# Logits of two heads side by side: 64-row products, one head in each half of the array

## The chip, the cores and the metric

The kernel runs on one core of a Trainium2 chip. The metric is the device time of one execution in microseconds (us). The core has a matrix engine (TensorE, PE in the profile, with its weight loads shown apart as PEld), a vector engine (VectorE, DVE), a scalar engine (ScalarE, ACT), a general engine (GpSimd, POOL) and a queue engine that starts transfers (SyncE, SP). Products accumulate in PSUM; everything else works in SBUF. The engines run beside each other and wait for one another by semaphores; each takes its own instructions in order.

## The reference

The kernel computes a trunk of two layers on x of 2048 frames by 1024 channels, in float32. Each layer normalises x, projects it, runs two groups of attention heads beside each other, multiplies each output by its SiLU gate, projects the concatenation and adds the residual.

- Group A (layer 0): differential attention, 4 heads. Each head has two sets of queries and keys of 64 numbers; the output uses softmax 1 minus lambda times softmax 2, with values of 128 numbers. A query sees all chunks up to its own, with a linear distance bias.
- Group B (layer 0): 8 heads of 64 with a forget gate, frame-causal; the logit bias is a difference of cumulated log gates.
- Group C (layer 1): 8 query heads on 2 key heads, a window of 128 frames, with sinks.
- Group D (layer 1): 8 heads of 64; a query sees its own chunk of 64 and the eight before it, with a learned bias by distance.

For A, B and D the core is the same:

```python
s = jnp.einsum("bqhd,bkhd->bhqk", qb, k).astype(jnp.float32) * scale
s = s + cq[..., :, None] - cum[:, :, None, :]
s = jnp.where(tk[None, :] <= tq[:, None], s, -jnp.inf)
p = jax.nn.softmax(s, axis=-1)
return jnp.einsum("bhqk,bkhd->bqhd", p.astype(v.dtype), v)
```

Queries and keys are RMS-normalised per head. The logits must be accurate beyond float16, so the kernel splits each operand into a high and a low float16 part and sums products of parts.

## The kernel before, in words

Frames are cut into 16 blocks of 128. The work is a list of steps, one per unit and block. A unit is one head of A (its two sets of queries and keys count as two heads below), or two heads of B, or two of D; so there are 4 units of A, 4 of B and 4 of D, each with 16 steps. Two units of C and the two output projections (32 steps) stand between and after them.

A step has parts, each a list of pieces with a cost in us that only serves to space them: the projection of its block (24 products of 512 columns: eight blocks of channels, three products of parts each, at lines 242 to 244), the split and transposition of queries and keys (`qk_prep`, lines 253 to 287), the logits with their softmax (`qk_row`, lines 322 to 367, and `exp_row`), and the products of the weights with the values (`heads_av`, line 407, for B and D; line 497 for A). The function `drive` runs these staggered: while step i forms its logits, step i+2 is projected, the transposes of step i+1 finish, and the weights of steps i-1 and i-2 meet the values. `merge` sorts the pieces of one turn by their share of the turn: the logits lie in the first nine tenths; B's and D's head 0 of step i-1 meets its values in the second half and head 1 of step i-2 in the first half; A's step i-2 in the first half. This, with the builder's ordering, sets the order of instructions on each engine. Transfers, the transposes of the weights among them, are started from SyncE's queue.

For queries and keys, `qk_prep` squares and sums, scales, and writes the parts high, low, high for every head (line 272 writes the high part twice on ScalarE, line 273 the low part on GpSimd). Pairs of neighbouring parts are transposed by TensorE: (high, low) of each key head, and (high, low) and (low, high) of each query head, six transposes of 128 columns, at lines 277 and 281; two copies on ScalarE bring keys (line 283) and queries (line 286) to SBUF. A key tile has two slots of 512 columns, one per head, with 64 rows of high parts above 64 rows of low parts. A logit of one head is therefore two products over all 128 rows (line 339): high x high + low x low, and low x high + high x low.

`qk_row` handles one head at a time. Its logits go to a PSUM tile of 1024 columns (two banks; there are two such tiles), in runs of up to four key blocks, which is one key tile. For B a further product with a causal mask follows on the last block (line 342). After up to eight blocks VectorE reduces the tile (line 351): it adds the bias, scales, writes the row to SBUF and keeps the running minimum of the negated logits, which goes on as a start value into the next reduction of the row. When the head's last reduction is issued, `exp_row` (line 374) takes the exponentials, and for B and D `weights_T` (lines 302 and 303) splits them into float16 parts and starts their transposition. Then the second head follows. For A both rows must be there first; VectorE and GpSimd combine them (lines 481 to 484) before `weights_T`. Rows live in six SBUF buffers of 1024 columns, shared with a few other uses.

For 16 key blocks a head has two rows of 1024 columns, so a step takes four of the six row buffers; for up to eight blocks, and always in D (at most five blocks), it has one row and the step takes two.

Of the kernel before, what the change touches and what calls it, by code (L numbers as in the profile page):

```python
# [9 lines left out]
F32 = mybir.dt.float32  # L10
F32R = mybir.dt.float32r
F16 = mybir.dt.float16
BF16 = mybir.dt.bfloat16
I32 = mybir.dt.int32
AF = mybir.ActivationFunctionType
ALU = mybir.AluOpType
# [43 lines left out]
class Trunk:  # L60
# [192 lines left out]
    def qk_prep(self, st, z, nq, nk, gain, kdst, mul=None):  # L253
# [13 lines left out]
        if nk:  # L267
            kn = zn[:, nq:, :]
            nc.gpsimd.tensor_tensor(out=kn, in0=kn, in1=gain[:, None, :].broadcast_to([P, nk, 64]), op=ALU.mult)  # L269

# [51 lines left out]
    def qk_row(self, row_st, q, ks, slot, kb0, m, bias, scale, last=None, diag=False):  # L322


        nc = self.nc
        pieces = []
        row_st["rows"] = []
        state = dict(prev=float(3e38))
        base = kb0 - kb0 % 4
        chunks = [(b, min(8, kb0 + m - b)) for b in range(kb0, kb0 + m, 8)]  # L330

        def mms(b0, b, n, end):
            if b == b0:
                state["ps"] = self.pS.tile([P, 1024], F32, tag="s", name="pss")
            c = (b - base) % 8 * P
            ps = state["ps"][:, c:c + n * P]
            k = ks[b // 4]
            for j in range(2):
                nc.tensor.matmul(ps, q()[:, j, :], k[:, slot, (b % 4) * P:(b % 4 + n) * P], start=(j == 0), stop=(j == 1 and not (end and diag)),  # L339
                                 skip_group_check=diag)  # L340
            if end and diag:
                nc.tensor.matmul(ps[:, n * P - P:], self.idh[:], self.causal[:], start=False, stop=True, skip_group_check=True)

        def row_of(b, n, first, last_chunk):
            if first:
                state["mx"] = self.sm.tile([P, 2], F32, tag="mx", name="mx")
            row = self.ap.tile([P, 1024], F32, tag="row", name="row", bufs=6)
            row_st["rows"].append((row, n))
            c = (b - base) % 8 * P
            mx = state["mx"][:, 0:1] if first else state["mx"][:, 1:2]  # L350
            nc.vector.tensor_tensor_reduce(  # L351
                out=row[:, :n * P], in0=state["ps"][:, c:c + n * P], in1=bias(b, n), op0=ALU.add, op1=ALU.min,
                scale=scale, scalar=state["prev"], accum_out=mx)
            state["prev"] = mx
            if last_chunk:
                self.exp_row(row_st, state["prev"])
                if last is not None:
                    last()
        for ci, (b0, n) in enumerate(chunks):
            lastc = ci == len(chunks) - 1  # L360
            b = b0
            while b < b0 + n:
                e = min((b // 4 + 1) * 4, b0 + n)
                pieces.append((2 * max((e - b) * P * 0.42e-3, 0.056), lambda b0=b0, b=b, e=e, x=lastc and e == b0 + n: mms(b0, b, e - b, x)))
                b = e
            pieces.append((0.0, lambda b0=b0, n=n, f=ci == 0, x=lastc: row_of(b0, n, f, x)))
        return pieces
# [58 lines left out]
    def unit_A(self, h, W, wsc, X):  # L426
# [3 lines left out]
        def mk(tb):  # L430
# [3 lines left out]
            def p():  # L434
# [8 lines left out]
                def post():  # L443
                    z = self.evac(st["z"], 512, wsc())
                    kd = self.ktile(ks, tb)
                    g = self.qk_prep(st, z, 2, 2, self.gA[h], kd)
                    if h == 0:
                        self.forget_gate(st, tb)
                    next(g)
                    vs.append(self.v_split(z[:, 256:384], wsc(), 1))  # L450
                    st["gate"] = self.silu2(z[:, 384:512], self.subg[:])
                    next(g)
                    st["fin"] = g
                return pieces + [(0.34, post)]

            def bias(b, n):
                off = (NT - 1 - tb + b) * P
                return self.distA[:, off:off + n * P]

            def q():  # L460
                self.two_sums(st, False)
                out = []
# [23 lines left out]
                for c in range(2):  # L486
                    out += self.qk_row(st["r"][c], lambda c=c: st["q"][c], ks, c, 0, m, bias, self.sA[:, 1 + h:2 + h], last if c == 1 else None)
                return out
# [28 lines left out]
    def unit_BD(self, kind, u, W, wsc, X):  # L517
# [17 lines left out]
        def mk(tb):  # L535
# [4 lines left out]
            def p():  # L540
# [6 lines left out]
                def post():  # L547
                    z = self.evac(st["z"], 512, wsc())
                    kd = self.ktile(ks, tb)
                    g = self.qk_prep(st, z, 2, 2, self.gB if kind == "B" else self.gD, kd)  # L550
# [8 lines left out]
            def bias(h, b, n):  # L559
                if kind == "D":  # L560
                    off = (5 - m + b - kb0) * P
                    return bias_t[h][:, off:off + n * P]
                return bias_t[b // 8, h][:, :n * P]

            def q():
                self.two_sums(st)
                out = []
# [6 lines left out]
                for h in range(2):  # L574
                    out += self.qk_row(st["r"][h], lambda h=h: st["q"][h], ks, h, kb0, m,
                                       lambda b, n, h=h: bias(h, b, n), (self.sB if kind == "B" else self.sD)[:, 1:2], last if h == 1 else None, kind == "B")
                return out
# [568 lines left out]
```

## Time and profile before

| | |
|---|---|
| median of 3 runs | 2675.35 us (2674.71 to 2675.85) |
| profiled execution | 2674.25 us, span 2672.5 us |
| TensorE busy | 2357.1 us, 88% of the span |
| VectorE busy | 1854.3 us, 69% |
| ScalarE busy | 1861.9 us, 70% |
| GpSimd busy | 1463.9 us, 55% |
| mean granted TensorE clock | 0.963 |

The stages in us from the start of the span: A to about 803, B to 1478, the first output projection to about 1700, C to 2005, D to 2486, the second output projection to the end. Busy shares are means over stages with different limits. A row of a group reads: line, engine, operation, output and inputs by the program's names, shapes, count, then busy time and mean ns of one, then the engine's idle time just before and what ended it. A row of waits reads: who waited for whom, total us, how often, the longest. TensorE's rows overlap each other, since products are pipelined, so their pace is read from the distance of starts in the timeline.

### The profile page before, as it was taken

What the parts mean: (1) busy time and instruction counts of PE and PEld (TensorE: products, weight loads), DVE (VectorE), ACT (ScalarE), POOL (GpSimd) and SP (SyncE); (2) the same over time, 40 slices, a digit from 0 to 9 for tenths busy, and PEclk for the clock granted to TensorE, in tenths of its full rate; (3) what the DMA queues carried; (4) which work ended last, traced back from release to release, by engine and by line L of the source; (5) the groups of instructions that cost most, each with busy time, mean ns of one, the idle gap of its engine ahead of it and who ended that gap; (6) DMA issues with size and microseconds to landing.
All of it is one profiled execution on the core that took longest, in us unless ns stands there. A gap on an engine that the chain in (4) does not pass through costs nothing. (4 is left out here: it accounts for less than half of the span.)

```text
span 2672.5 us, 53354 instructions
## 1 busy us (share of the span) xinstructions
PE 2357.1 (88%) x18448; PEld 1300.2 (49%) x18448; DVE 1854.3 (69%) x5228; ACT 1861.9 (70%) x4289; POOL 1463.9 (55%) x2311
## 2 busy tenths in 40 slices
PE   6778888988889989888995898899999999999799
PEld 2344544545455555445553433565555554555344
DVE  6677888888897867857767544566877676767431
ACT  6676777777777877868777444777987777777420
POOL 4555867777786555645554100656575767576300
PEclk9798999999999999999997999999999999999899
DMA  7756555445356997978879999444666776666983
GB/s 213 185 152 137 123 129 132 96 103 125 93 127 133 186 198 147 210 152 165 169 152 193 268 273 245 144 95 118 146 171 138 174 143 163 142 128 141 247 226 103
DMA packets 888208, 426.67 MB, mean 160 GB/s; under 512 B 785377, under 2 KB 816097, under 8 KB 887937
## 3 DMA queue, kind: packets, MB, share of 16 engines
q1 hardware_dynamic: 887936, 423.27, 69.2%
q8 instruction: 144, 2.36, 0.4%
q14 instruction: 128, 1.04, 0.1%
HBM read 187.68 MB, written 42.01 MB: 86 GB/s over the span
## 5 line engine op out<-in xcount | busy, mean ns | idle before, releaser
L374 ACT ACTIVATE row<-row,mx 128x1024 f32<-128x1024 f32 (+7 forms) x512 | 438.2, 857 | 113.2 <-DVE mx L351 111.1
L339 PE MATMUL pss<-kT,qT 128*128 128x512 f16 (+3 forms) x1728 | 398.1, 347 | 56.3 <-DVE mx L351 49.7
L303 DVE SCALAR_TENSOR_TENSOR ph<-row,ph 128x1024 f16<-128x1024 f32 (+6 forms) x320 | 285.6, 902 | 109.3 <-ACT ph L302 107.3
L242 PE MATMUL z<-w,xr 128*128 128x512 f16 x896 | 346.2, 388 | 16.2 <-DMA xr<-xhl 9.0
L242 PE MATMUL z<-w,x 128*128 128x512 f16 x896 | 342.9, 383 | 11.6 <-DMA x<-xs 10.5
L243 PE MATMUL z<-w,xr 128*128 128x512 f16 x896 | 347.2, 388 | 3.4 <-POOL w L113 1.9
L244 PE MATMUL z<-w,xr 128*128 128x512 f16 x896 | 346.4, 387 | 0.0
L243 PE MATMUL z<-w,x 128*128 128x512 f16 x896 | 342.4, 382 | 0.0
L244 PE MATMUL z<-w,x 128*128 128x512 f16 x896 | 342.2, 382 | 0.0
L121 POOL TENSOR_TENSOR y<-v,mhalf 128x4 f32<-128x4 f32 (+2 forms) x329 | 308.4, 938 | 9.1
L407 PE MATMUL OT<-V,pT 128*128 128x64 f16 x5688 | 237.0, 196 | 79.5 <-DMA pT<-ph 77.4
L407 PEld LDWEIGHTS <-pT 128*128 128x128 f16 x5688 | 215.7, 100 | 147.5 <-DMA pT<-ph 96.9
L302 ACT ACTIVATE ph<-row 128x1024 f16<-128x1024 f32 (+6 forms) x320 | 234.4, 744 | 64.0 <-DMA pT<-ph 59.0
L339 PEld LDWEIGHTS <-qT 128*128 128x128 f16 x1728 | 153.1, 101 | 185.9 <-issue 75.7
L273 POOL TENSOR_TENSOR hl<-zs,hl 128x256 f16<-128x256 f32 (+1 forms) x240 | 177.6, 740 | 101.1 <-ACT hl L272 99.2
L123 DVE TENSOR_TENSOR q<-y 128x4 f32<-128x4 f32 (+2 forms) x329 | 90.6, 276 | 204.3 <-POOL y L121 202.4
L272 ACT ACTIVATE hl<-zs 128x512 f16<-128x512 f32 (+1 forms) x240 | 145.8, 608 | 58.9 <-POOL zs L269 52.9
L250 ACT ACTIVATE zs<-z,sc 128x512 f32<-128x512 f32 (+1 forms) x240 | 158.2, 661 | 25.3 <-PE z L244 25.0
L242 PE MATMUL zo<-w,xm 128*128 128x512 f16 x352 | 137.9, 392 | 31.7 <-DVE res L727 14.0
L176 ACT ACTIVATE wrn<-wrn,lng 128x512 f32<-128x512 f32 (+1 forms) x112 | 78.6, 702 | 108.4 <-DMA wrn<-in_wd_dram 43.3
L497 PE MATMUL OA<-V,pT 128*128 128x128 f16 x1632 | 117.4, 230 | 40.6 <-DMA pT<-ph 34.7
L113 POOL TENSOR_TENSOR w<-wraw,w 128x512 f16<-128x512 f32 x118 | 145.6, 1237 | 11.3 <-ACT w L109 10.6
(225 smaller groups left out, 5562.7 us busy)
## 6 DMA issues: line engine op xcount, KB each, us to landing
x<-xs SPq DMA_DIRECT2D x112, 512.0 KB, 3.8
wraw<-in_w_dram SPq DMA_DIRECT2D x64, 256.0 KB, 3.0
wrn<-in_w_dram SPq DMA_DIRECT2D x56, 256.0 KB, 2.9
x<-in_x_dram SPq DMA_DIRECT2D x16, 512.0 KB, 5.1
xs<-xt SPq DMA_DIRECT2D x16, 512.0 KB, 3.3
mixa<-out SPq DMA_DIRECT2D x128, 64.0 KB, 2.1
biasB<-cumd SPq DMA_DIRECT2D x32, 256.0 KB, 5.1
wrn<-in_wo_dram SPq DMA_DIRECT2D x32, 256.0 KB, 3.3
```

The source lines that it names most:

```text
L121: nc.gpsimd.tensor_tensor(out=y[:], in0=v[:], in1=self.mhalf[:, :n], op=ALU.pow)
L242: nc.tensor.matmul(ps(), xh, wh, start=(kb == 0), stop=False)
L243: nc.tensor.matmul(ps(), xh, wl, start=False, stop=False)
L244: nc.tensor.matmul(ps(), xl, wh, start=False, stop=(kb == KB - 1))
L250: self.nc.scalar.activation(zs[:, :n], z[:, :n], AF.Copy, scale=sc[:, 0:1])
L272: nc.scalar.activation(hl[:, :, 0::2], zn[:, :, None, :].broadcast_to([P, n, 2, 64]), AF.Copy)
L273: nc.gpsimd.tensor_tensor(out=hl[:, :, 1], in0=zn, in1=hl[:, :, 0], op=ALU.subtract)
L302: nc.scalar.activation(hl[:, :n], w, AF.Copy, scale=scale)
L303: nc.vector.scalar_tensor_tensor(out=hl[:, n:2 * n], in0=w, scalar=scale, in1=hl[:, :n], op0=ALU.mult, op1=ALU.subtract)
L339: nc.tensor.matmul(ps, q()[:, j, :], k[:, slot, (b % 4) * P:(b % 4 + n) * P], start=(j == 0), stop=(j == 1 and not (end and diag)), skip_g ...
L374: nc.scalar.activation(row[:, :hm * P], row[:, :hm * P], AF.Exp, scale=-1.0, bias=nmax, accum_out=s[:, i:i + 1])
L407: nc.tensor.matmul(O[:, head], w()[:, a], V()[:, b], start=first and a + b == 0, stop=last and a == 1, skip_group_check=True)
```

## The change

Logits of two heads are formed together. `qk_prep`, called with a new argument for A, B and D (not C), writes each part once: the high parts of all four heads (two of queries, two of keys) and then the low parts. One transpose turns the same part of both heads of a pair, so there are four in place of six; head 0 lands in rows 0 to 63 and head 1 in rows 64 to 127, and the second index of the key and query tiles is the part and not the head. The copy of the queries is half as wide.

The function `qk_rows` takes the place of `qk_row`. A PSUM tile is now two banks of 512 columns, one for each head, and holds one run of up to four key blocks of both. Each run has three products of parts (high x high, high x low, low x high; low x low is left out), and each is issued for head 0 on rows 0 to 63 and for head 1 on rows 64 to 127: six products of 64 rows. The causal product of B stays a product of 128 rows, one per head. After each run both heads are reduced, so a reduction covers at most 512 columns and continues from the head's last minimum. The rows keep their 1024 columns. Head 0's exponentials are issued with its last reduction, right before head 1's last reduction; the spacing costs are three products per run in place of two per head and run.

```diff
+        if pairs:
+
+            hl = ap.tile([P, 2, n, 64], F16, tag="hl", name="hl", bufs=2)
+            nc.scalar.activation(hl[:, 0], zn, AF.Copy)
+            nc.gpsimd.tensor_tensor(out=hl[:, 1], in0=zn, in1=hl[:, 0], op=ALU.subtract)
+            yield
+
+            pt = self.pT.tile([P, 4, P], F16, tag="t", name="ptq")
+            for s in (1, 0):
+                for a in range(2):
+                    nc.tensor.transpose(pt[:, 2 * s + a], hl[:, a, 2 * s:2 * s + 2].rearrange("p h d -> p (h d)"), self.idh[:])
+            nc.scalar.activation(kdst, pt[:, 2:], AF.Copy)
+            qT = ap.tile([P, 2, P], F16, tag="qT", name="qT", bufs=2)
+            nc.scalar.activation(qT[:], pt[:, :2], AF.Copy)
+            st["q"] = qT
+            return
...
-    def qk_row(self, row_st, q, ks, slot, kb0, m, bias, scale, last=None, diag=False):
...
+    def qk_rows(self, row_st, q, ks, kb0, m, bias, scale, last, diag=False):
+
+
+        nc = self.nc
+        for r in row_st:
+            r["rows"] = []
+        state = [dict(prev=float(3e38)) for _ in range(2)]
+        ps = {}
+
+        def mms(b, n, end):
+            t = ps[b] = self.pS.tile([P, 2, 512], F32, tag="s", name="pss")
+            k, o = ks[b // 4], (b % 4) * P
+            for i, (a, c) in enumerate(((0, 0), (0, 1), (1, 0))):
+                for h in range(2):
+                    s = slice(64 * h, 64 * h + 64)
+                    nc.tensor.matmul(t[:, h, :n * P], q()[s, a], k[s, c, o:o + n * P], start=(i == 0), stop=(i == 2 and not (end and diag)),
+                                     skip_group_check=True)
+            if end and diag:
+                for h in range(2):
+                    nc.tensor.matmul(t[:, h, n * P - P:n * P], self.idh[:], self.causal[:], start=False, stop=True, skip_group_check=True)
+
+        def row_of(h, b, n, end):
+            r, s = row_st[h], state[h]
+            first = b == kb0
+            if first:
+                s["mx"] = self.sm.tile([P, 4], F32, tag="mx", name="mx")
+                s["n"] = 0
+            if (b - kb0) // 8 == len(r["rows"]):
+                r["rows"].append([self.ap.tile([P, 1024], F32, tag="row", name="row", bufs=6), 0])
+            at = r["rows"][-1]
+            mx = s["mx"][:, s["n"]:s["n"] + 1]
+            s["n"] += 1
+            nc.vector.tensor_tensor_reduce(
+                out=at[0][:, at[1] * P:(at[1] + n) * P], in0=ps[b][:, h, :n * P], in1=bias(h, b, n), op0=ALU.add, op1=ALU.min,
+                scale=scale, scalar=s["prev"], accum_out=mx)
+            at[1] += n
+            s["prev"] = mx
+            if end:
+                self.exp_row(r, mx)
+                if h == 1:
+                    last()
         pieces = []
...
+        b = kb0
+        while b < kb0 + m:
+            e = min((b // 4 + 1) * 4, kb0 + m)
+            pieces.append((3 * max((e - b) * P * 0.42e-3, 0.056), lambda b=b, e=e: mms(b, e - b, e == kb0 + m)))
+            for h in range(2):
+                pieces.append((0.0, lambda h=h, b=b, e=e: row_of(h, b, e - b, e == kb0 + m)))
+            b = e
         return pieces
...
-                for c in range(2):
-                    out += self.qk_row(st["r"][c], lambda c=c: st["q"][c], ks, c, 0, m, bias, self.sA[:, 1 + h:2 + h], last if c == 1 else None)
-                return out
+                return self.qk_rows(st["r"], lambda: st["q"], ks, 0, m, bias, self.sA[:, 1 + h:2 + h], last)
...
-                return bias_t[b // 8, h][:, :n * P]
+                return bias_t[b // 8, h][:, b % 8 * P:(b % 8 + n) * P]
...
-                for h in range(2):
-                    out += self.qk_row(st["r"][h], lambda h=h: st["q"][h], ks, h, kb0, m,
-                                       lambda b, n, h=h: bias(h, b, n), (self.sB if kind == "B" else self.sD)[:, 1:2], last if h == 1 else None, kind == "B")
-                return out
+                return self.qk_rows(st["r"], lambda: st["q"], ks, kb0, m, bias, (self.sB if kind == "B" else self.sD)[:, 1:2], last, kind == "B")
```

More of the change, by code (lines that the diff above doesn't have):

```diff
@@ L251, in evac, with qk_prep @@
         return zs
-    def qk_prep(self, st, z, nq, nk, gain, kdst, mul=None):
+    def qk_prep(self, st, z, nq, nk, gain, kdst, mul=None, pairs=False):
         nc, ap = self.nc, self.ap
@@ L319, in silu2 @@
         return g
-    def qk_row(self, row_st, q, ks, slot, kb0, m, bias, scale, last=None, diag=False):
+    def qk_rows(self, row_st, q, ks, kb0, m, bias, scale, last, diag=False):
         nc = self.nc
-        pieces = []
[L327 to L366, printed above, removed]
@@ L445, in post @@
                     kd = self.ktile(ks, tb)
-                    g = self.qk_prep(st, z, 2, 2, self.gA[h], kd)
+                    g = self.qk_prep(st, z, 2, 2, self.gA[h], kd, pairs=True)
                     if h == 0:
@@ L454, in p, with bias @@
                 return pieces + [(0.34, post)]
-            def bias(b, n):
+            def bias(c, b, n):
                 off = (NT - 1 - tb + b) * P
@@ L461, in q @@
                 self.two_sums(st, False)
-                out = []
                 def last():
@@ L549, in post @@
                     kd = self.ktile(ks, tb)
-                    g = self.qk_prep(st, z, 2, 2, self.gB if kind == "B" else self.gD, kd)
+                    g = self.qk_prep(st, z, 2, 2, self.gB if kind == "B" else self.gD, kd, pairs=True)
                     next(g)
@@ L562, in bias @@
                     return bias_t[h][:, off:off + n * P]
-                return bias_t[b // 8, h][:, :n * P]
+                return bias_t[b // 8, h][:, b % 8 * P:(b % 8 + n) * P]
             def q():
                 self.two_sums(st)
-                out = []
                 def last():
```

## The prediction

> **What bounds the kernel now.** I read the head of the page first, then stretches of time, then the waits, then single lines. The profiled execution took 2674.25 us, its span is 2672.5 us, and 1.75 us lie around it; the median of the runs shown is 2675.35 us, so the sum below is made against 2674.25 and can be read against the median without a shift.
>
> ```profile
> span 2672.5 us, 53354 instructions
> PE 2357.1 (88%) x18448; PEld 1300.2 (49%) x18448; DVE 1854.3 (69%) x5228; ACT 1861.9 (70%) x4289; POOL 1463.9 (55%) x2311
> ```
>
> The 88% is an average. The next table has busy time by stretch: first the stages A, B and D (the three that the change touches), then four half units: rows of A and B with at most 8 key blocks (639 to 710, 1305 to 1376) and with 9 to 16 (710 to 806, 1039 to 1132).
>
> ```profile
> core 0: us, PE busy (x) PEld busy (x) DVE busy (x) ACT busy (x) POOL busy (x), PEclk, DMA share, GB/s
> 52.00:803.00 751.00, 632.50 (x4285) 348.92 (x4286) 614.46 (x1750) 544.43 (x1284) 518.14 (x779) 0.94 0.53 128
> 803.00:1478.00 675.00, 589.95 (x5847) 338.27 (x5845) 499.27 (x1214) 519.69 (x1117) 370.61 (x570) 0.96 0.84 172
> 2005.00:2486.00 481.00, 450.89 (x3890) 254.26 (x3888) 333.33 (x953) 368.18 (x878) 317.87 (x545) 0.98 0.70 149
> ...
> 639.00:710.00 71.00, 66.00 (x496) 37.57 (x495) 59.43 (x199) 51.16 (x134) 51.40 (x88) 1.00 0.44 96
> 710.00:806.00 96.00, 81.13 (x562) 45.44 (x560) 88.08 (x222) 74.51 (x169) 72.75 (x101) 0.96 0.49 121
> 1039.00:1132.00 93.00, 82.12 (x868) 47.00 (x867) 77.36 (x171) 77.30 (x158) 55.79 (x79) 1.00 0.88 188
> 1305.00:1376.00 71.00, 69.92 (x670) 39.91 (x669) 46.76 (x139) 53.57 (x127) 35.71 (x65) 0.99 0.75 143
> ```
>
> TensorE leads in D (451 of 481 us) and in the early halves (66.0 and 69.9 of 71). In the late half of A it does not: VectorE is busy 88.1 of 96 us, TensorE 81.1. In the late half of B three things stand close together, VectorE and ScalarE at 77 of 93 and the DMA engines at 0.88. The waits say the same: TensorE's own stops are for VectorE's row reductions and for transposed weights.
>
> ```profile
> PE OT L407 <- DMA pT<-ph: 77.4, 57, 5.2
> PE pss L339 <- DVE mx L351: 49.7, 45, 3.4
> PE OA L497 <- DMA pT<-ph: 34.7, 25, 3.1
> ```
>
> **Logit products.** The old row function issues four 128-row products per pair of heads and run of up to four key blocks; the new one issues six 64-row products, three per head.
>
> ```profile
> L339 PE MATMUL pss<-kT,qT 128*128 128x512 f16 (+3 forms) x1728 | 398.1, 347 | 56.3 <-DVE mx L351 49.7
> ...
> 245.05 0.38 PE L243 MATMUL z<-w,xr 128*128 128x512 f16 x1
> 245.26 0.38 PE L244 MATMUL z<-w,xr 128*128 128x512 f16 x1
> 245.57 1.04 PE L742 MATMUL psf<-x,wf 128*16 128x256 f16 x8
> 246.55 0.82 PE L339 MATMUL pss<-kT,qT 128*128 128x512 f16 x3
> ...
> 147.71 0.38 PE L244 MATMUL z<-w,x 128*128 128x512 f16 x1
> 148.02 0.23 PE L749 MATMUL psf<-idf,fg 16*128 16x16 f32 x1
> ...
> 1158.97 0.39 PE L281 MATMUL ptq<-idh,hl 128*128 128x128 f16 x4
> 1159.20 0.38 PE L243 MATMUL z<-w,x 128*128 128x512 f16 x1
> ```
>
> Durations of TensorE rows overlap, so I price by starts: 512 columns take 0.216 us (245.05 to 245.26), 0.422 ns a column. The loops give 1728 / 4 = 432 runs (40 in each of eight units of A and B, 28 in each of four of D): 252 of 512 columns and 60 each of 384, 256 and 128, together 175,104 columns. Four passes are 295.5 us. If the two halves of the array work at the same time, three passes are 221.6 us, a gain of 73.9. If they work one after another, six passes are 443.3 us, a loss of 147.7. No row of this trace has two products in different rows of the array, so these are the ends. I take the overlapped one: the trace's nearest product, the 16-row L749, leaves the array's other rows unused, and the two halves' inputs, weights and accumulators (a bank for each head) are disjoint. By the Trainium skill, TensorE: Matmul & The Clock Gate, Part 3, products in different row groups start about 4 ns apart; by that the three passes are estimated at 5 us more, and no run here shows it yet.
>
> **Entering and leaving the 64-row form.** The rows above show a price. From L244 to the 16-column L742 the start is 0.31 us later instead of 0.216: 0.093. The eight products of 256 columns (0.108 us each by the column price, 0.87) hold the engine 0.98 us until L339 starts: 0.1 on the way out. The 16-row L749 is entered at the same price (147.71 to 148.02). I take 0.093 us in and out for a 64-row product too; the bounds are 0 and 0.1. With 432 runs, each between 128-row work (in B the causal product at L342 follows at once), that is 80 us at most; some runs will adjoin or start after a stop, and I take nine in ten, 72 us. By the Trainium skill, TensorEngine Tiling (Array Packing), Key Properties, changing the tiling mode drains the engine, while changing only the tile does not. It makes 64 rows a mode of its own, which no row here shows; by it these 72 us are due, without it TensorE's sum is better by them.
>
> **Transposes.** Six per step become four, in 64 steps of each kind, 192 in all: 384 fewer at 0.057 us (four in 1158.97 to 1159.20), 22 us off TensorE. TensorE's sum: −73.9 − 22 + 72 = −24 us. It counts where TensorE leads, in D and the early halves, about half of the three stages: **−12 us**, with 0 and −24 as ends.
>
> **Row reductions on VectorE.** This is the term that I think decides. The old function reduces up to 1024 columns of one head at once, the new one at most 512, since a tile now holds two heads.
>
> ```profile
> L351 DVE CUSTOM_DVE_ANT_0 row<-pss,distA,gA3s x128: 329/1271/1285, 52.4 to 799.5; 128x1024 f32<-128x1024 f32 x72, 128x128 f32<-128x128 f32 x8, 128x256 f32<-128x256 f32 x8, 128x384 f32<-128x384 f32 x8
> L351 DVE CUSTOM_DVE_ANT_0 row<-pss,distA,mx x64: 396/870/1344, 157.4 to 801.0; 128x128 f32<-128x128 f32 x8, 128x256 f32<-128x256 f32 x8, 128x384 f32<-128x384 f32 x8, 128x512 f32<-128x512 f32 x8
> L351 DVE DVE_READ_ACCUMULATOR2_ANT mx<- 128x1 f32 x512 | 41.0, 80 | 0.0
> ```
>
> From 128 columns (329 ns) to 1024 (1271) a column costs 1.05 ns and the instruction 194 ns beside them. A reduction that continues from an earlier minimum costs 67 more (396 against 329), and each is followed by a read of 80 ns. So a row cut once more costs 194 + 67 + 80 = 0.341 us without doing more. Reductions go from 512 to 2 x 432 = 864: 352 more, 120 us of VectorE: 128 each in A and B (43.6 us), 96 in D (32.7). Of A's, 24 per unit lie in the late half: 8.2 us on 88.1 busy in a stretch of 96. Even without a gap VectorE would then need 96.3. I take 6 us for each of four units (ends 0 and 8.2): **+24**. The late half of B has 16 us of VectorE idle time, but ScalarE and the DMA engines beside it: 4 of 8.2 a unit, **+16**. Early halves have 8 more reductions, 2.7 us, under TensorE's cover; if that cover went, all of it would be due. I take 0.5 in each of eight: **+4**. D hides nearly all of 32.7 behind TensorE (VectorE 333 of 481): **+3**.
>
> **Split and copies.** The fp16 parts are no longer doubled.
>
> ```profile
> L272 ACT ACTIVATE hl<-zs 128x512 f16<-128x512 f32 x224 | 139.4, 623 | 55.8 <-POOL zs L269 51.7 <-DVE zs L266 3.6
> L258 ACT ACTIVATE sq<-zs 128x256 f32<-128x256 f32 x224 | 91.7, 409 | 2.0
> L286 ACT ACTIVATE qT<-ptq 128x512 f16<-128x512 f16 x192 | 112.6, 587 | 0.3 <-PE pss L339 0.3
> L283 ACT ACTIVATE kT<-ptq 128x256 f16<-128x256 f16 x208 | 76.9, 370 | 43.7 <-PE ptq L281 39.6 <-PE ptq L277 3.9
> ```
>
> By the 256-column rows the split falls from 623 to about 409 ns and the copy of q from 587 to 370, together 0.431 us x 192 = 83 us of ScalarE. It leads nowhere, so I count only **−5** for earlier keys and queries (ends 0 and −20). GpSimd's subtraction keeps its 256 elements.
>
> **Rows grow together.** Head 0's exponentials used to run in the middle of a step; now all follow the last reduction.
>
> ```profile
> L374 ACT ACTIVATE row<-row,mx 128x1024 f32<-128x1024 f32 x160 | 182.6, 1142 | 48.4 <-DVE mx L351 47.3 <-DVE rs L386 0.9
> L374 ACT ACTIVATION_READ_ACCUMULATOR row<-row,mx 128x1 f32 x512 | 97.4, 190 | 0.0
> L302 ACT ACTIVATE ph<-row,cf 128x1024 f16<-128x1024 f32 x40 | 45.8, 1144 | 43.6 <-POOL row L482 36.4 <-DVE cf L475 4.4 <-POOL V L113 1.3
> L303 DVE SCALAR_TENSOR_TENSOR ph<-row,cf,ph 128x1024 f16<-128x1024 f32 x40 | 52.7, 1318 | 5.4 <-ACT ph L302 5.1
> ...
> L482 POOL TENSOR_TENSOR row<-row x64: 448/1263/1720, 101.8 to 812.2; 128x512 f32<-128x512 f32 x40, 128x128 f32<-128x128 f32 x8, 128x256 f32<-128x256 f32 x8, 128x384 f32<-128x384 f32 x8
> ...
> DVE row L351 <- POOL row L482: 12.6, 8, 3.1
> ```
>
> At 16 blocks two more exponentials of 1.33 us stand between a step's last logit and its first transposed weights: 2.7 us. What is queued behind them on ScalarE are the evacuation of the next projection and the split; what waits for them are the output products L497 and L407, which already stop 34.7 and 77.4 us. The products come a step or more later, so most is covered: I take **+8** (ends 0 and 86, 2.7 us in 32 late steps of A). Sum: −12 + 24 + 16 + 4 + 3 − 5 + 8 = +38, so 2674 + 38 = 2712; I say 2710.
>
> **Rivals.** (1) The halves do not overlap. Then the change does not do what its words say: TensorE gets 147.7 − 22 + 72 = +198 us, a tenth of it in its own stops: 2674 + 180 = **2855**. For it: no row shows overlap. Against: nothing shared between the halves. (2) The row buffers close a loop. Six buffers of 1024 columns serve four per late step, so the second pair of a step needs the first pair of the step before. After the change a loop runs through four exponentials (5.3 us), GpSimd's combination at L482 (1.3), the copy (1.1) and subtraction (1.3), and four reductions of the next step (each 396 + 384 x 1.05 + 80 ns, together 3.5): 12.5 us, and a late step of A lasts 96 / 8 = 12. The wait on L482, 12.6 us now, would grow by some 1.5 us in each of the 32 late steps: 48 on top of 2712, **2760**. Against: the loop is only just as long as a step. (3) On the other side: faster, because the drains fall into stops. TensorE already stops before logits (56.3 us by L339), and a drain there is free. With 20 us of drains left, TensorE's sum is −76, of which some 45 count in the early halves and D, and VectorE absorbs more than half of its load (+20): 2674 − 45 + 20 = about **2650**. It decides if over half of the 432 runs begin after a stop. Against: in D hardly any do. (4) VectorE's extra work disappears in its idle time and TensorE gains nothing: **2674**.
>
> **How the numbers follow.** Forecast 0.43 (own range 2685 to 2740), rival 1 0.10, rival 2 0.13, rival 3 0.24, rival 4 0.10. What a measurement can tell from no change is about 0.2%, 5 us. So faster 0.24, same 0.10, slower 0.43 + 0.10 + 0.13 = 0.66. The range 2640 to 2790 leaves out rival 1 and the lower part of rival 3, some 0.2.
>
> **What would show it.** Overlap: starts of the two heads' products nearly together and the next pair 0.216 us later; if they start 0.216 apart, rival 1. Drains: 0.31 us instead of 0.216 at the border of a run. VectorE: 864 reductions and some 120 us more busy time, with the late half of A near 97%; if that stretch isn't longer, my main term is wrong. Row buffers: the wait of L351's successor on GpSimd's row above 12.6 us. ScalarE: about 80 us less. A late half of B that shrinks would make the sign wrong.

## The result and the profile after

The changed kernel takes 2723.45 us, median of 4 runs (2720.29 to 2724.51), against 2675.6 us before: a ratio of 1.0177, 95% interval 1.016 to 1.0195, so 48 us slower. The forecast was 2710 in a range of 2640 to 2790. The direction and the rough size came out as forecast; the step that was to decide the time did not, as the runs below show.

Head of the page of the changed kernel (span; busy time, share and instructions of each engine):

```profile
span 2722.1 us, 55058 instructions
PE 2376.4 (87%) x18928; PEld 1218.8 (45%) x18928; DVE 1921.1 (71%) x5932; ACT 1786.4 (66%) x4289; POOL 1475.0 (54%) x2311
```

VectorE is busy 67 us more, ScalarE 76 less, TensorE 19 more. No engine is busy all the time. The mean granted clock is 0.952 against 0.963; the second form of the first experiment below was granted 0.953 and takes as long as the kernel before, so the lower clock by itself does not explain the loss.

Stretches of the changed kernel (columns as in the prediction): A, B, D; the last unit of A from the end of its eighth step to the end of its last, each ending with the reciprocal that normalises its output; and the same for the third unit of B.

```profile
core 0: us, PE busy (x) PEld busy (x) DVE busy (x) ACT busy (x) POOL busy (x), PEclk, DMA share, GB/s
55.00:825.00 770.00, 636.41 (x4500) 317.85 (x4499) 641.25 (x2019) 521.51 (x1291) 520.24 (x785) 0.92 0.52 126
825.00:1523.00 698.00, 601.20 (x6029) 310.06 (x6027) 515.98 (x1441) 493.95 (x1109) 376.79 (x564) 0.94 0.80 165
2045.00:2544.00 499.00, 457.81 (x3986) 232.91 (x3985) 353.19 (x1146) 344.68 (x874) 323.00 (x544) 0.97 0.68 146
709.00:825.00 116.00, 97.40 (x710) 47.85 (x709) 101.39 (x303) 80.70 (x192) 84.74 (x118) 0.93 0.52 120
1235.00:1347.00 112.00, 97.87 (x1043) 50.91 (x1044) 88.10 (x244) 80.18 (x175) 63.30 (x93) 0.97 0.78 167
```

The same two half units of the kernel before:

```profile
697.00:806.00 109.00, 93.17 (x648) 52.03 (x647) 97.39 (x251) 83.25 (x190) 80.00 (x113) 0.97 0.48 117
1196.00:1305.00 109.00, 95.90 (x961) 55.31 (x960) 85.79 (x189) 83.98 (x173) 63.51 (x91) 0.94 0.89 173
```

A is 19 us longer (751 to 770), B 23 (675 to 698), D 18 (481 to 499; 23 if both are cut at the same instruction), the rest some 10 shorter. In the late half unit of A VectorE is at 87% (101.4 of 116), where the forecast had 97%; before it was at 89% (97.4 of 109). Measured between these reciprocals, the late halves of A's four units together take 481 us for 479 before, those of B 459 for 440; the early halves, where TensorE led, 289 for 272 and 239 for 234. D lost as much as A, though VectorE has 146 us of idle time there.

Groups and waits of the changed kernel: the logit products; TensorE's three largest waits; the reductions that continue a row, with the wait for a row buffer; the reads behind reductions; and the split with its copy.

```profile
L353 PE MATMUL pss<-kT,qT 64*128 64x512 f16 (+3 forms) x2592 | 326.4, 353 | 52.8 <-DVE mx L370 47.9
...
PE OT L427 <- DMA pT<-ph: 93.8, 76, 6.9
PE pss L353 <- DVE mx L370: 47.9, 34, 7.4
PE OA L514 <- DMA pT<-ph: 40.8, 30, 4.0
...
L370 DVE CUSTOM_DVE_ANT_0 row<-pss,distA,mx 128x512 f32<-128x512 f32 x120 | 93.1, 803 | 13.9 <-POOL row L501 10.8 <-PE pss L353 2.5
L370 DVE DVE_READ_ACCUMULATOR2_ANT mx<- 128x1 f32 x864 | 69.6, 81 | 0.0
...
L273 ACT ACTIVATE hl<-zs 128x256 f16<-128x256 f32 x192 | 78.3, 408 | 77.1 <-POOL zs L269 76.6
L283 ACT ACTIVATE qT<-ptq 128x256 f16<-128x256 f16 x192 | 71.6, 373 | 0.0
```

TensorE waits as long for reductions as before (47.9 us, and 49.7 before), and longer for transposed weights: 93.8 and 40.8 us against 77.4 and 34.7.

TensorE around two runs of logit products (start, us of the group, engine, line, ..., count):

```profile
1087.07 0.38 PE L244 MATMUL z<-w,x 128*128 128x512 f16 x1
1087.28 0.38 PE L242 MATMUL z<-w,x 128*128 128x512 f16 x1
1087.60 0.66 PE L353 MATMUL pss<-kT,qT 64*128 64x384 f16 x6
1088.19 0.29 PE L357 MATMUL pss<-causal,idh 128*128 128x128 bf16 x2
1088.31 0.38 PE L243 MATMUL z<-w,x 128*128 128x512 f16 x1
...
1091.04 0.82 PE L353 MATMUL pss<-kT,qT 64*128 64x512 f16 x6
1091.80 0.55 PE L427 MATMUL OT<-V,pT 128*128 128x64 f16 x13
```

Six products of 512 columns hold TensorE 0.75 us up to the next start, the way out included: three passes, so the halves overlap. The six start at 0, 3, 226, 230, 442 and 445 ns. The price of entering shows at 1087.60: 0.32 us after L242, not 0.216.

From the starts of all products I split TensorE's span: products at their columns' price (0.4167 ns a column, four times that in float32, and 2.5 ns a product; within a 64-row run the measured distance of starts), excess at the borders of 64-row runs, gaps of more than 0.3 us beyond the product ahead ("stops"), and small gaps. All tables of TensorE below are worked out in this way, in us:

| | before | after |
|---|---|---|
| logit products | 296.2 | 245.8 |
| borders, in + out | 0 | 42.9 + 37.5 |
| other products | 1941.5 | 1920.0 |
| small gaps | 83.3 | 78.1 |
| stops | 333.4 | 378.8 |

By this account the logits with their borders cost 30 us more instead of 2 less, the transposes 21.5 less, and **the stops grew by 45**: nearly the whole loss. Why they grew is what the runs were for.

### The profile page after: what moved, and what is told of

Same layout as the page of the kernel before. It is cut to its first block, busy times and chain, and to the rows that moved or that the text cites. A ratio compares the mean times of both kernels' runs of the same rounds, so it can differ in the third digit from the quotient of the medians.

```text
span 2722.1 us, 55058 instructions
## 1 busy us (share of the span) xinstructions
PE 2376.4 (87%) x18928; PEld 1218.8 (45%) x18928; DVE 1921.1 (71%) x5932; ACT 1786.4 (66%) x4289; POOL 1475.0 (54%) x2311
## 5 line engine op out<-in xcount | busy, mean ns | idle before, releaser
L353 PE MATMUL pss<-kT,qT 64*128 64x512 f16 (+3 forms) x2592 | 326.4, 353 | 52.8 <-DVE mx L370 47.9
L242 PE MATMUL z<-w,xr 128*128 128x512 f16 x896 | 349.9, 392 | 15.2 <-DMA xr<-xhl 8.9
L242 PE MATMUL z<-w,x 128*128 128x512 f16 x896 | 345.7, 386 | 11.1 <-DMA x<-xs 8.1
L427 PE MATMUL OT<-V,pT 128*128 128x64 f16 x5688 | 234.1, 196 | 97.0 <-DMA pT<-ph 93.8
L427 PEld LDWEIGHTS <-pT 128*128 128x128 f16 x5688 | 204.8, 100 | 180.3 <-DMA pT<-ph 120.4
L274 POOL TENSOR_TENSOR hl<-zs,hl 128x256 f16<-128x256 f32 x192 | 153.2, 798 | 67.7 <-ACT hl L273 66.7
L353 PEld LDWEIGHTS <-qT 64*128 64x128 f16 x2592 | 100.1, 96 | 186.3 <-issue 114.6
L310 POOL TENSOR_SCALAR zs<-zs,sc 128x128 f32<-128x128 f32 x208 | 100.5, 483 | 123.1 <-ACT zs L250 122.4
L242 PE MATMUL zo<-w,xm 128*128 128x512 f16 x352 | 137.4, 390 | 20.8 <-DVE res L740 8.6
L514 PE MATMUL OA<-V,pT 128*128 128x128 f16 x1632 | 116.4, 229 | 43.3 <-DMA pT<-ph 40.8
```

Of the source, the lines that this page charges most:

```text
L242: nc.tensor.matmul(ps(), xh, wh, start=(kb == 0), stop=False)
L274: nc.gpsimd.tensor_tensor(out=hl[:, 1], in0=zn, in1=hl[:, 0], op=ALU.subtract)
L353: nc.tensor.matmul(t[:, h, :n * P], q()[s, a], k[s, c, o:o + n * P], start=(i == 0), stop=(i == 2 and not (end and diag)), skip_group_chec ...
L427: nc.tensor.matmul(O[:, head], w()[:, a], V()[:, b], start=first and a + b == 0, stop=last and a == 1, skip_group_check=True)
```

## The experiments

**Shorter reductions alone.** The kernel before, head by head, with each reduction cut to one run of at most 512 columns. In the first form the PSUM tile stays at 1024 columns; in the second each run has a tile of one bank, four of them.

```diff
+                pieces.append((0.0, lambda b0=b0, b=b, e=e, x=lastc and e == b0 + n: row_of(b0, b, e - b, x)))
...
-            pieces.append((0.0, lambda b0=b0, n=n, f=ci == 0, x=lastc: row_of(b0, n, f, x)))
...
```

The second form has this besides, and four buffers in that pool in place of two:

```diff
-            if b == b0:
-                state["ps"] = self.pS.tile([P, 1024], F32, tag="s", name="pss")
+            state[b] = self.pS.tile([P, 512], F32, tag="s", name="pss")
...
```

Expected of the first:

> The kernel before, head by head with 128-row products, but every row is reduced in pieces of at most 512 columns: 864 reductions for 512, some 120 us more of VectorE and nothing else. If the cut reductions are the main cause of the changed kernel's +48 us, this takes 2710 to 2725 us. If the drains or the late exponentials are, it stays under 2685.

Measured: 2773.79, ratio 1.0353 (1.0316 to 1.039), far beyond what was expected. Waits of this kernel:

```profile
PE pss L339 <- DVE mx L354: 105.5, 126, 3.5
```

That wait was 49.7 us before. The products of a row's second run go to the tile whose first half is still being reduced, and wait; the second form shows that this is the tile's price and not the cut's. Expected of the second form:

> As the first cut of the rows, but every run of up to four blocks has a PSUM tile of its own (four of one bank in place of two of two), since in the first version the second run's products waited for the first run's reduction (810 waits for VectorE on logit products, 441 before). If the cut itself is the cost, this stays above 2740; if the waits inside a tile were, it falls to the 2685 of the kernel with both heads together.

Measured: 2682.06, ratio 1.001 (0.9997 to 1.0023). Page and waits of this kernel:

```profile
PE 2377.6 (89%) x18448; PEld 1307.3 (49%) x18448; DVE 1908.9 (71%) x5932; ACT 1862.7 (70%) x4289; POOL 1460.5 (55%) x2311
...
PE pss L337 <- DVE mx L351: 57.3, 55, 3.4
```

It has the 704 extra VectorE instructions of the change (x5932, 5228 before) and 55 us more VectorE time, and takes as long as before: 3 us more, with an interval from 1 us less to 6 us more. **The cut costs nothing that can be measured.**

**Both heads together, old products.** The change with the old split, six transposes and four products of 128 rows per run. Its spacing cost is four products per run, as in the kernel before (two per head); the lines that set it and the calls of the old split are left out here.

```diff
-            for i, (a, c) in enumerate(((0, 0), (0, 1), (1, 0))):
-                for h in range(2):
-                    s = slice(64 * h, 64 * h + 64)
-                    nc.tensor.matmul(t[:, h, :n * P], q()[s, a], k[s, c, o:o + n * P], start=(i == 0), stop=(i == 2 and not (end and diag)),
-                                     skip_group_check=True)
+            for h in range(2):
+                for j in range(2):
+                    nc.tensor.matmul(t[:, h, :n * P], q()[h][:, j], k[:, h, o:o + n * P], start=(j == 0), stop=(j == 1 and not (end and diag)),
+                                     skip_group_check=True)
...
```

> The changed kernel's order (both heads' rows grow together, reductions of at most 512) with the old split, the old six transposes and the old 128-row products, four per run. If the cut reductions alone decide, it takes what the cut alone takes, within 10 us. If it costs that rows are finished together and all exponentials come late, it is over 20 us slower than the cut alone.

Measured: 2684.73, ratio 1.0031 (1.0014 to 1.0049), +8 us for the cut and the joint rows. The last unit of A's late half in this kernel:

```profile
703.00:812.00 109.00, 91.68 (x660) 52.50 (x658) 98.56 (x303) 84.44 (x193) 82.45 (x118) 0.96 0.54 127
```

The same 303 VectorE instructions as after the change, but 109 us as before it, not 116. (All four late halves of A take 485 us here, 479 before and 481 after the change, so a single one is rough.)

**The border by itself.** A 64-row product of one column ahead of head 0's products in each run of the kernel before, and ahead of each run of the kernel just shown.

```diff
+            if slot == 0:
+                nc.tensor.matmul(ps[:, 0:1], q()[0:64, 0, :], k[0:64, slot, (b % 4) * P:(b % 4) * P + 1], start=True, stop=True, skip_group_check=True)
...
```

And in the joint form:

```diff
+            nc.tensor.matmul(t[:, 0, 0:1], q()[0][0:64, 0], k[0:64, 0, o:o + 1], start=True, stop=True, skip_group_check=True)
...
```

> The kernel before with one more product of 64 rows and one column ahead of each of head 0's 432 runs; its result is overwritten. It adds the border between the two forms twice, 432 x (0.096 + 0.092 + about 0.03) us = 94 us of TensorE, and no other work. If TensorE's time counts where it leads (half of the three stages), 2715 to 2735; if most of it falls into stops, 2680 to 2700.

Measured: 2694.5, ratio 1.0061 (1.0045 to 1.0077).

> Both heads together with 128-row products and cut reductions (2685 us), plus the 64-row product of one column ahead of each run: cut reductions and drains at once, without the gains of the change. If the two are hidden by the same idle time, over 2720: more than the sum of their own costs (+8 and +18 give 2702). If they add up, 2695 to 2710, and the rest of the changed kernel's loss is in its products or its new split.

Measured: 2701.25, ratio 1.0081 (1.0057 to 1.0105). The timeline of the first of the two:

```profile
1107.86 0.25 PE L409 MATMUL OT<-V,pT 128*128 128x64 f16 x3
1108.04 0.17 PE L339 MATMUL pss<-kT,qT 64*128 64x1 f16 x1
1108.15 0.60 PE L341 MATMUL pss<-kT,qT 128*128 128x512 f16 x2
```

TensorE got 40.7 us of borders in, 33.7 out and 12.1 of products, 86.5 together; its stops shrank from 333 to 278, its small gaps by 10, and the kernel grew by 16 (0.0061 x 2676.6). About a fifth came through. On the joint rows it is 0.005, 13 us for 85: the same within the intervals. So the borders take TensorE about as long as forecast. That most of it only fills time in which TensorE would have waited fits the shorter stops, but is not shown by these two alone: the builder ordered them anew, and of TensorE's 16592 other products 2423 stand in another place than in the kernel before, 1794 in the joint form.

**A wide tile for each head.** The 64-row products with a tile of 1024 columns for each head and reductions uncut, a row's two runs issued together; then the same with the six products of a run held in their order.

```diff
-            t = ps[b] = self.pS.tile([P, 2, 512], F32, tag="s", name="pss")
+            if b == b0:
+                ps[b0] = [self.pS.tile([P, 1024], F32, tag="s", name="pss") for _ in range(2)]
...
+            t = [x[:, at:at + n * P] for x in ps[b0]]
...
```

> The changed kernel, but each head has a PSUM tile of its own of 1024 columns, so a row is reduced up to 1024 at once as before (512 reductions), and the runs of up to eight blocks are issued together: 256 borders for 432. PSUM holds no second pair of tiles then. If cut reductions and drains are the cause, TensorE is 96 us lighter less 48 us of drains and VectorE as before: 2640 to 2670. If the late exponentials are the cause, over 2700; if the missing second pair of tiles stops TensorE, over 2700 with longer waits of the logit products on VectorE's minimum.

Measured: 2762.83, ratio 1.032 (1.0301 to 1.034). Timeline of this kernel:

```profile
1106.22 1.47 PE L358 MATMUL pss<-kT,qT 64*128 64x512 f16 x6
1107.62 0.55 PE L438 MATMUL OT<-V,pT 128*128 128x64 f16 x13
```

Six products take 1.40 us: one after another. Only 619 of 1296 pairs start within some 10 ns of each other (1185 after the change): the builder often puts the two runs of one head, six products of the same half, ahead of the other head's. The likely reason, not tested, is that the two tiles come free at different times.

The same with the products held in order, by a dependency that costs the chip no wait:

```diff
+                    for ins in nc.cur_bb.bb.instructions[i0:]:
+                        if ins.engine == mybir.EngineType.PE:
+                            if i + h:
+                                self.tc.add_manual_dep(ins, prev.name, chained, reason="pair")
+                            prev = ins
...
```

> The kernel with a tile of 1024 columns per head, with the six products of a run held in the order of the change by edges that cost nothing at run time; without them the builder had set one head's products after the other's and only 619 of 1296 pairs overlapped. If the lost overlap made it slow, it gains the missing 677 passes, some 110 us of TensorE, and takes 2650 to 2700. If the missing second pair of tiles made it slow, it stays over 2740.

Measured: 2813.51, ratio 1.0489 (1.0467 to 1.051), with 1012 overlapping pairs. Waits of this kernel:

```profile
PE pss L360 <- DVE mx L381: 69.7, 54, 4.7
```

More overlap and still slower. Two tiles per row leave no second pair in PSUM, and the products wait longer for the reductions, 69.7 us against 47.9 after the change. That is 22 of the 84 us (1.0489 less 1.0177) by which this kernel is slower than the change; the rest is not explained, nor is why more overlap came with more time. Neither kernel says anything on the cut, which the second form above tested alone.

**Order of the six products.** The change with head 0's three products ahead of head 1's in program order.

```diff
-            for i, (a, c) in enumerate(((0, 0), (0, 1), (1, 0))):
-                for h in range(2):
+            for h in range(2):
+                for i, (a, c) in enumerate(((0, 0), (0, 1), (1, 0))):
```

> The changed kernel with the three products of head 0 ahead of the three of head 1, the rest in the same order: five passes for three, about +140 us of TensorE. If TensorE's time sets the end, 2830 to 2865; if the stops absorb it, as with the added drains (a fifth came through), 2740 to 2770.

Measured: 2726.73, ratio 1.017 (1.0155 to 1.0186), no different from the change. Timeline of this kernel:

```profile
1091.16 0.83 PE L353 MATMUL pss<-kT,qT 64*128 64x512 f16 x6
1091.92 0.55 PE L427 MATMUL OT<-V,pT 128*128 128x64 f16 x13
```

The run takes 0.76 us and not 1.40: the halves overlap although the program doesn't alternate them (nor does the built program: three products of one half stand ahead of three of the other). So this isn't the undoing of the overlap that it was meant to be; the next kernel is.

**No overlap.** Both heads' products on rows 0 to 63, so that head 1's logits are those of head 0.

```diff
-                    s = slice(64 * h, 64 * h + 64)
+                    s = slice(0, 64)
```

> The changed kernel with the products of both heads on rows 0 to 63, so that nothing can overlap and six passes are run one after another, in the same order; head 1's logits are then those of head 0. It adds 222 us of TensorE at most. If TensorE's time sets the end, 2900 or more; if about a fifth comes through, as with the added drains, 2760 to 2790.

Measured: 2764.47, ratio 1.0334 (1.0309 to 1.036). Timeline, then waits of this kernel:

```profile
1106.92 1.47 PE L353 MATMUL pss<-kT,qT 64*128 64x512 f16 x6
1108.32 0.55 PE L427 MATMUL OT<-V,pT 128*128 128x64 f16 x13
...
PE OT L427 <- DMA pT<-ph: 41.1, 36, 6.0
PE OA L514 <- DMA pT<-ph: 20.2, 17, 4.0
```

The logits take TensorE 471 us instead of 246, 225 more; the kernel takes 0.0157 or 42 us more, 19% of it. The stops fall from 379 to 208, those for transposed weights from 93.8 and 40.8 to 41.1 and 20.2. So overlap saves about 42 us here, and about a fifth of TensorE's time comes through. This is the cleanest pair of all: the two traces show the same instructions in the same order on every engine, so nothing but the time of these products differs.

**Split and rows as changed, products of 128 rows.** The new split, four transposes, joint rows and cuts, with four products over all 128 rows per run. Its logits are sums over both heads, and its spacing cost is four products per run, where the change has three.

```diff
-            for i, (a, c) in enumerate(((0, 0), (0, 1), (1, 0))):
-                for h in range(2):
-                    s = slice(64 * h, 64 * h + 64)
-                    nc.tensor.matmul(t[:, h, :n * P], q()[s, a], k[s, c, o:o + n * P], start=(i == 0), stop=(i == 2 and not (end and diag)),
-                                     skip_group_check=True)
+            for h in range(2):
+                for j in range(2):
+                    nc.tensor.matmul(t[:, h, :n * P], q()[:, j], k[:, h, o:o + n * P], start=(j == 0), stop=(j == 1 and not (end and diag)),
+                                     skip_group_check=True)
-            pieces.append((3 * max((e - b) * P * 0.42e-3, 0.056), lambda b=b, e=e: mms(b, e - b, e == kb0 + m)))
+            pieces.append((4 * max((e - b) * P * 0.42e-3, 0.056), lambda b=b, e=e: mms(b, e - b, e == kb0 + m)))
```

> The changed kernel's split, transposes and row order, but four 128-row products per run in place of six of 64 rows, so no border between forms. Each product then sums over both heads: the logits are not those of the reference, the work of every other engine is. If the new split is what is left of the loss, 2695 to 2710; if the borders and the 64-row products are, 2670 to 2688.

Measured: 2687.72, ratio 1.0052 (1.0032 to 1.0072). Page of this kernel:

```profile
PE 2350.0 (88%) x18064; PEld 1281.9 (48%) x18064; DVE 1909.5 (71%) x5932; ACT 1778.4 (66%) x4289; POOL 1475.5 (55%) x2311
```

ScalarE's relief is in it (84 us less than before) and 22 us of transposes, and it is no faster than the joint rows with the old split. All but the 64-row products and their spacing costs 14 us (0.0052); **the step to the 64-row products, with the builder's new order, costs the other 33** (1.0177 less 1.0052). On TensorE:

| | 128-row products | after | all on rows 0 to 63 |
|---|---|---|---|
| logit products | 296.2 | 245.8 | 471 |
| borders | 0 | 80.4 | 84 |
| small gaps | 90.3 | 78.1 | 67.8 |
| stops | 356.2 | 378.8 | 207.5 |

By a fifth of TensorE's +30 the step from the first column to the second should cost 6 us, with shorter stops. It costs 33, and the stops get longer by 23. Most of that lies ahead of the products with the values, which wait for transposed weights; waits of the kernel with 128-row products:

```profile
PE OT L426 <- DMA pT<-ph: 82.8, 85, 6.0
PE OA L513 <- DMA pT<-ph: 37.3, 28, 2.9
```

After the change these are 93.8 and 40.8 us, 14 us more. Two simpler reasons can be left out: the transposes of queries and keys are stopped for as long in both kernels (55 and 56 us), and VectorE's reductions wait no longer for their logits (36 and 32 us).

**Two guesses at the stops.** The low parts transposed first, as the last transposes were thought to hold the logits up; and the logits' spacing cost raised from three products to four, as the new cost puts less room around a run.

```diff
-                for a in range(2):
+                for a in (1, 0):
```

The other kernel:

```diff
-            pieces.append((3 * max((e - b) * P * 0.42e-3, 0.056), lambda b=b, e=e: mms(b, e - b, e == kb0 + m)))
+            pieces.append((4 * max((e - b) * P * 0.42e-3, 0.056), lambda b=b, e=e: mms(b, e - b, e == kb0 + m)))
```

> The changed kernel with the transposes of the low parts ahead of those of the high parts. In the change a high part can be transposed as soon as ScalarE has written it; the builder then puts that transpose early, and TensorE, which goes in order, stops there and again for GpSimd's low part (stops ahead of these transposes: 60 us in the changed kernel, 28 to 33 in the kernels with the old split). If these stops are the part of the loss that the drains leave open, it takes 2695 to 2705; if not, 2715 to 2730.

Measured: 2737.5, ratio 1.0232 (1.0206 to 1.0258); stops 389.

> The changed kernel with one number changed: a run's logit piece counts as four products for the spacing of the pieces, as in the kernels with 128-row products, and not as three. It moves no work, only the order in which the builder issues it. If the order is what makes the changed kernel's stops longer than those of the kernels that were spaced with four, 2690 to 2705; if the 64-row products themselves are, 2715 to 2730.

Measured: 2742.86, ratio 1.0243 (1.0221 to 1.0266); stops 387. Neither guess helped: each kernel got slower. With the same work on every engine, three orders give 2723, 2737 and 2743 us. In the two new ones 2523 and 2339 of TensorE's 16208 products other than logits stand in another place than in the change; between the kernel with 128-row products and the change it is 3205.

Two things follow. The last kernel is spaced with four products per run, as the one with 128-row products is; with the spacing held, the step to 64-row products costs 51 us (1.0243 less 1.0052) and not 33. And wherever the order differs, a difference of some 15 to 20 us can be the order's alone. That holds for all kernels here but two, those with the order of the six products changed and with all products on rows 0 to 63, which keep the change's order on every engine.

## Why the prediction was right, and where it was wrong

**Row reductions on VectorE (+47 of the sum's +38).** This step failed. Its count and price were right: 864 reductions, and the durations of reductions and reads sum to 124 us more, where 120 were forecast. The inference was wrong: that the late half of A had no room. Part of it is a misread border: the stretch from 710 us begins after the step of nine blocks, whose reductions start at 699, so it holds seven of the eight late steps. Over all eight (697 to 806) VectorE is busy 97.4 of 109 us, and 11.6 us were free for the 8.2. Cut alone, the reductions move the time by 0.1% (interval through 0), the late half of A's last unit took 109 us with all of them in the joint form, and after the change the late halves of A are 2 us longer in all, not 24. Three kernels have all 864 reductions, one run to a tile, and products of 128 rows alone; they are 3, 8 and 14 us slower than before. Each has an order of its own, but a cost of 47 us is not in them. With the change A lost 19 us, B 23 and D 18; the step had +24, +16 and +3 for A's late halves, B's and D. B's late halves did lose 19 us, but with joint rows and cuts alone they lost nothing (435 us for 440).

**Logit products and borders (−2).** Overlap came, at 3 to 4 ns between the starts of a pair, as the Trainium skill has it (TensorE: Matmul & The Clock Gate, Part 3). The price of a border was right: 96 ns in and 92 out, 80 us in all for 72. The passes were mis-sized: 246 us for 221.6. There are 450 stretches of 64-row work for 432 runs, and 111 pairs didn't start together. So the term is +30, not −2. By the run's length: 512 columns take 850 ns with the ways in and out, for 864 before; 384 take 690 for 650; 256, 530 for 438; 128, 370 for 224. Only the longest gains.

**Transposes (−22)**: 21.5, by the same column price. **What TensorE's sum is worth (half, −12)**: the pair with the order held shows a fifth (42 of 225 us), and the sum is +8 instead of −24.

**ScalarE (−5)**: 76 us less busy for 83 forecast; with the new split the joint rows are no faster, so 0 is nearer.

**Rows together (+8)**: +8 together with the cut, which alone has +3. Right in size, as far as the order's share allows to say.

**Rivals.** (1) No overlap: refuted; it was made, and gives 2764, not 2855, since the forecast took nine tenths of TensorE's time to come through. (2) Row buffers: the wait is 10.8 us, 12.6 before; refuted by the trace alone, as no other number of buffers was tried. With the right border a late step lasts 109 / 8 = 13.6 us, longer than the loop of 12.5, so the rival's own sum had no case. (3) Drains in stops: half right. Added TensorE time does displace stops (171 of 225 us where the order is held), but the stops of the changed kernel are longer than before. (4) VectorE's work disappears: true; but the time isn't 2674.

So 2710 came out near 2723 by luck: 47 us were put down to a cost that isn't there, and 33 us (51 with the spacing held) came with the 64-row products, which were to gain. **Open** is why the stops lengthen with them. The joint rows, cut, split and transposes together account for 14 us. The 64-row products' own time on TensorE is 30 us more, which at a fifth is 6. The remaining 27 us may be the order: the builder orders the instructions by what it expects of each, a fifth of TensorE's other products (3205 of 16208) changes place with the 64-row products, and two other orders of the same work moved the time by 14 and 19 us. So the order is large enough to be most of it, but this is argued and not shown: no run here holds the order while 64-row products take the place of 128-row ones.

## What to carry to other kernels

Products in two halves of the array pay for a change of form on each side, so count columns per stay in the form: here three passes for four gain 14 ns of 864 at 512 columns and lose below. Whether longer stays would pay is open. Before a busy share is turned into a cost, add that work alone and see: 55 us more of VectorE cost nothing that can be measured, and TensorE, busy 87% of the span, passed on a fifth of 225 us. Compare the order of instructions in the two traces too: where a builder reorders, only a pair with the same order gives the price of one thing. Give each reduction a PSUM tile of its own when it is cut: 105.5 us of waits in a shared tile, 57.3 with a tile each.

## What the runs showed of the hardware

- Products on rows 0 to 63 and 64 to 127 run beside each other even if the program has three of the one ahead of three of the other: starts at 0, 10, 226, 236, 442 and 452 ns, 761 ns for the run against 754 alternated. With all six on rows 0 to 63 the starts lie 216 to 226 ns apart, so two that start 10 ns apart are one of each half. The Trainium skill (TensorE: Matmul & The Clock Gate, Part 3) has products start in program order; here the fourth in the program starts ahead of the second.
- Entering and leaving the 64-row form costs about the same as the 16-row and 16-column forms of the trace before (93 ns): 96 and 92 ns in the median. Ahead of a product of a single column it is 96 ns too; that product and the way out take 106 ns together. The Trainium skill (TensorEngine Tiling (Array Packing), Key Properties) says that changing the tiling mode drains TensorE; the trace agrees, at these prices.
- Added TensorE time came through at a fifth where nothing else differed: 225 us more of logit products made this kernel 42 us longer, and TensorE's stops 171 us shorter.
